# Up and gate products of three feed-forward layers by Strassen's scheme, their weight sums made by adding DMAs, in a one-core transformer kernel

## Chip, cores and metric

One core of a Trainium2 chip runs the whole kernel. The metric is the device time of one execution in microseconds (us); of several runs the median counts. PE is TensorE (matrix products), DVE VectorE, ACT ScalarE, POOL GpSimd, and SP SyncE, which issues the loads.

## What is computed

A two-layer diffusion trunk in float32 over 256 latent tokens (lat) and 256 context tokens (ctx), width D = 1024. Every layer is a half-step SwiGLU feed-forward (FFN), a token mixer, and a second FFN, each on normalised tokens with scale, shift and gate from a modulation vector:

```python
def swiglu(z, w13, w2):
    gate, up = jnp.split(z @ w13, 2, axis=-1)
    return (jax.nn.silu(gate) * up) @ w2
...
    for l in range(DEPTH):
        m_l = (s_lat @ mod_w[l] + mod_b[l]).reshape(b, N_MOD, 1, d)
        m_c = (s_ctx @ mod_w[l] + mod_b[l]).reshape(1, N_MOD, 1, d)
        h = h + 0.5 * m_l[:, 2] * swiglu(modulate(h, norm_g[l, 0], m_l[:, 0], m_l[:, 1]), ffn_w13[l, 0], ffn_w2[l, 0])
        hc = hc + 0.5 * m_c[:, 2] * swiglu(modulate(hc, norm_g[l, 0], m_c[:, 0], m_c[:, 1]), ffn_w13[l, 0], ffn_w2[l, 0])
```

The hidden width is 2816, which is 22 tiles of 128. The FFNs are named (layer, which): (0,0), (0,1) and (1,0) have all 512 tokens, (1,1) has the 256 latent ones. The mixer of layer 0 joins a spatial gate and grouped-query attention; that of layer 1 is a matrix LSTM. The modulation weights `mod_w` are 1024 x 9216 for each layer.

## The kernel before

Features lie on partitions, tokens on the free axis. Each float32 product is made of three matmuls of a faster type: every operand is split into a high and a low part, and `mm3` (lines 106 to 110) adds hi·hi, hi·lo and lo·hi. Weights come by loads that SP issues in program order into `raw` (pool `rawp`, four buffers of 1 MB). `wsplit` takes 128 x 1024 elements: ACT casts the high part (`whi`, line 102), DVE subtracts it to get the low part (`wlo`, line 103). The pool `whp` holds four such splits. A load waits until its buffer has been read, a cast until its `whi` buffer has been used by PE.

In `ffn` the work of an FFN with 512 tokens is:

- Column pairs: 11 values of `cc`, each with 256 columns of gate and 256 of up. A hidden tile of 128 columns takes 8 feature blocks x 3 matmuls of 128x512 for gate, and as many for up; so a column pair has 96 such matmuls. `hidden` (lines 518 to 521) makes silu(gate)·up and splits it into `hh` and `hl`.
- The first column pair of the FFNs (0,1) and (1,0) is done in two halves of 256 tokens, since the context half of `z` is ready later. Pieces of the norm before lie between its products (`poke`, `settle`).
- The second product, `w2`: four passes `dp` of 256 output columns over all 22 hidden tiles; the last pass in two token halves. `resid` (line 399) adds the result to `hT`.

DVE has a filler that lies between the other work: `mod_round_dve` makes 512 columns of the modulation (a round) out of two 1 MB loads by 16 DVE operations, then PE sums over the partitions (line 267). `fill` issues one eighth of a round, two operations; `tick` says how many eighths come per step, from `FILL`. `LEAD` lets the scheduler put the filler early.

The engines each run their queue in order; a scheduler sets the order ahead of time, from the order in which the code is written and from its priorities. The FFNs stand in this order:

```python
    filler.extend([(0, r) for r in range(4, 18)] + [(1, r) for r in range(18)])
    nxt = Next(0, 1)
    until[0] = (0, 17)
    ffn(0, 0, z, T, [(0, T)], nxt, fill13=FILL[0][0], fill2=FILL[0][1], first=first)
```

## Time and profile before

| what | value |
|---|---|
| time, median of 3 runs (lowest to highest) | 1754.0 us (1753.57 to 1755.47) |
| span of the profiled execution | 1753.2 us |
| PE busy | 1732.7 us, 99% |
| DVE busy | 1126.9 us, 64% |
| ACT busy | 635.0 us, 36% |
| POOL busy | 88.1 us, 5% |
| mean granted TensorE clock | 0.997 |
| moved by DMA | 256.90 MB, 147 GB/s |

The span runs from the first to the last instruction of the profiled execution. The lowest of the three times lies 0.4 us above it, the median 0.8 us. Matmuls are pipelined: in the rows each lasts longer than the distance to the next, and the distance is what a matmul costs in a row of them.

### The profile page before, as it was taken

To read this page: it belongs to the slowest core of one execution; us is meant where nothing else is said; L and a number is where in the kernel's file an instruction comes from. 1 tells how busy PE (TensorE), PEld (TensorE's weight loads), DVE (VectorE), ACT (ScalarE), POOL (GpSimd) and SP (SyncE) were. 2 spreads that over 40 slices of the span, in tenths; PEclk is the share of its full clock that TensorE was granted. 3 is DMA by queue.
4 is the path that set the end of the run, shared out by engine and by line. 5 is a ranking of instruction groups with operands and counts; after the bars stand their busy time and mean duration, and the time that the engine had idled before them with its cause. 6 is when DMAs were issued, how large, how long until landed. Compare 5 with 4: busy or idle time off the path is not lost.

```text
span 1753.2 us, 25482 instructions
## 1 busy us (share of the span) xinstructions
PE 1732.7 (99%) x10359; PEld 1470.2 (84%) x10359; DVE 1126.9 (64%) x1968; ACT 635.0 (36%) x1028; POOL 88.1 (5%) x109
## 2 busy tenths in 40 slices
PE   7999999999999999999999999999999999999998
PEld 5777777779988987777777987777889999899998
DVE  5677777767775676675676766663334965695554
ACT  4322222224665332222222432222223564364442
POOL 0000000001542000000000000000000001100000
PEclk9999999999999999999999999999999999999999
DMA  9655555555211234445454455443224432146552
GB/s 281 216 194 172 174 191 172 179 189 174 73 49 49 97 129 164 164 144 190 141 182 163 159 168 168 144 162 121 88 87 118 146 114 79 49 130 207 190 178 67
DMA packets 234937, 256.90 MB, mean 147 GB/s; under 512 B 9288, under 2 KB 201028, under 8 KB 234820
## 3 DMA queue, kind: packets, MB, share of 16 engines
q1 hardware_dynamic: 234788, 255.27, 45.0%
q8 instruction: 81, 1.33, 0.3%
q14 instruction: 36, 0.29, 0.1%
q10 hardware_dynamic: 32, 0.01, 0.0%
HBM read 254.21 MB, written 1.05 MB: 146 GB/s over the span
## 4 chain that ended last, share of the span: by engine, by line
PE 84%; issue 11%; DVE 2%; DMA 1%; ACT 1%; SPq 0%; POOL 0%; POOLq 0%; DVEq 0%; ACTq 0%
PE ps L108 23%; PE ps L110 23%; PE ps L109 23%; PE ps L659 2%; PE ps L660 2%; PE ps L661 2%; PE mod_ps L267 2%; DMA mod<-in_mod_w_dram 1%; PE nd_ps L1353 1%; PE pv_ps L995 1%; PE sc_ps L950 1%; PE nd_ps L1350 1%; PE prT_ps L113 1%; DVE wlo L103 1%; PE mod_ps L219 0%
## 5 line engine op out<-in xcount | busy, mean ns | idle before, releaser
L102 ACT CAST whi<-raw 128x1024 fp32r<-128x1024 f32 (+1 forms) x338 | 346.7, 1027 | 900.4 <-PE ps L109 792.8
L103 DVE TENSOR_TENSOR wlo<-raw,whi 128x1024 fp32r<-128x1024 f32 (+1 forms) x338 | 401.6, 1193 | 278.3 <-ACT whi L102 276.4
L108 PE MATMUL ps<-zhi,whi 128*128 128x512 f32 (+2 forms) x1616 | 575.3, 357 | 1.6 <-ACT zhi L366 1.6
L110 PE MATMUL ps<-zhi,wlo 128*128 128x512 f32 (+2 forms) x1616 | 574.2, 356 | 0.0
L109 PE MATMUL ps<-zlo,whi 128*128 128x512 f32 (+2 forms) x1616 | 573.4, 355 | 0.0
L108 PEld LDWEIGHTS ps<-zhi,whi 128*128 128x128 f32 x1616 | 304.6, 189 | 57.8 <-issue 10.6
L109 PEld LDWEIGHTS ps<-zlo,whi 128*128 128x128 f32 x1616 | 304.9, 189 | 46.2 <-issue 0.4
L110 PEld LDWEIGHTS ps<-zhi,wlo 128*128 128x128 f32 x1616 | 304.3, 189 | 44.6 <-issue 0.6
L258 DVE SCALAR_TENSOR_TENSOR mod_acc<-raw,s_st,mod_acc 128x512 f32<-128x512 f32 x448 | 305.7, 744 | 11.4 <-DMA raw<-in_mod_w_dram 11.3
L108 PE MATMUL ps<-hh,whi 128*128 128x256 f32 (+1 forms) x836 | 281.8, 337 | 0.0
L110 PE MATMUL ps<-hh,wlo 128*128 128x256 f32 (+1 forms) x836 | 281.7, 337 | 0.0
L109 PE MATMUL ps<-hl,whi 128*128 128x256 f32 (+1 forms) x836 | 280.8, 336 | 0.0
L110 PEld LDWEIGHTS ps<-hh,wlo 128*128 128x128 f32 x836 | 157.4, 188 | 21.9 <-issue 4.9
L108 PEld LDWEIGHTS ps<-hh,whi 128*128 128x128 f32 x836 | 157.5, 188 | 20.9 <-issue 4.1
L109 PEld LDWEIGHTS ps<-hl,whi 128*128 128x128 f32 x836 | 157.5, 188 | 19.6 <-issue 2.5
L519 DVE TENSOR_TENSOR sil<-sil,ps 128x512 f32<-128x512 f32 (+1 forms) x85 | 52.9, 623 | 139.9 <-PE ps L110 139.0
L659 PE MATMUL ps<-whi,zhi 128*128 128x256 f32 x288 | 82.4, 286 | 1.4 <-DVE cy L1056 1.4
L660 PE MATMUL ps<-wlo,zhi 128*128 128x256 f32 x288 | 80.8, 281 | 0.0
L661 PE MATMUL ps<-whi,zlo 128*128 128x256 f32 x288 | 80.8, 281 | 0.0
L119 POOL TENSOR_TENSOR rs<-rs,mhalf 128x2 f32<-128x2 f32 x12 | 8.5, 710 | 1069.0 <-DVE rs L118 1069.0
L659 PEld LDWEIGHTS ps<-whi,zhi 128*128 128x128 f32 x288 | 54.1, 188 | 2.6 <-ACT whi L102 1.8
L660 PEld LDWEIGHTS ps<-wlo,zhi 128*128 128x128 f32 x288 | 54.2, 188 | 0.4
(290 smaller groups left out, 1520.2 us busy)
## 6 DMA issues: line engine op xcount, KB each, us to landing
raw<-in_ffn_w_dram SPq DMA_DIRECT2D x103, 1024.0 KB, 5.3
raw<-in_mod_w_dram SPq DMA_DIRECT2D x64, 1024.0 KB, 7.4
raw<-in_ffn_w_dram SPq DMA_DIRECT2D x38, 896.0 KB, 5.0
raw<-in_ml_w_in_dram SPq DMA_DIRECT2D x12, 1024.0 KB, 5.7
mod<-in_mod_w_dram SPq DMA_DIRECT2D x16, 512.0 KB, 7.5
raw<-in_ab_w_in_dram SPq DMA_DIRECT2D x7, 1024.0 KB
raw<-in_ml_w_out_dram SPq DMA_DIRECT2D x4, 1024.0 KB, 5.5
raw<-in_ffn_w_dram SPq DMA_DIRECT2D x8, 256.0 KB, 3.0
```

Source lines behind the costliest of these rows:

```text
L102: act.copy(hi, view)
L103: dve.tensor_tensor(lo, view, hi.bitcast(F32), op=ALU.subtract)
L108: pe.matmul(ps, ah, bh, start=start, stop=False)
L109: pe.matmul(ps, ah, bl, start=False, stop=False)
L110: pe.matmul(ps, al, bh, start=False, stop=stop)
L113: pe.transpose(out_ps, in_sb, ident[:n, :n])
L258: dve.scalar_tensor_tensor(acc[:, v], raw[:, k], s1, acc[:, v], op0=ALU.mult, op1=ALU.add)
L267: pe.matmul(ps[32 * j : 32 * (j + 1), :256], onehot[:, MAXG - 1 - m : MAXG + 31 - m], acc[:, v, hf * 256 : (hf + 1) * 256], start=(m == 0) ...
L519: dve.tensor_tensor(sil[:, :N], sil[:, :N], pu[:, :N], op=ALU.mult)
L659: pe.matmul(o, zh, wh[:, k % 4], start=(k == 0), stop=False)
L660: pe.matmul(o, zh, wl[:, k % 4], start=False, stop=False)
L661: pe.matmul(o, zl, wh[:, k % 4], start=False, stop=(k == KD - 1))
```

## The change

For the three FFNs with 512 tokens `ffn512` takes the place of `ffn`. From the second column pair on (in (0,0) from the fourth), the 256 columns of gate and of up, the two halves of the features and the two halves of the tokens form a 2 x 2 block product. It is made of seven block products instead of eight (a form of Strassen's scheme): 28 column pairs in all. A block product is 24 matmuls of 128x256 (4 feature blocks x 3 parts x 2 column tiles). So a column pair has 168 matmuls of 128x256.

For that the weights need sums of blocks: a1, S3, S2 and S4 stand one after the other in the same half of the buffer `rsum`. Each is split, and then POOL issues a DMA that loads the next block from memory and adds it in place (two DMAs of 256 KB for a sum, six for a column pair). S1 is added on DVE, from the other half of `rsum` and from `rpl`, which holds the blocks a2 and g2 as they are. The tokens need sums too (`combos_lat`, `combos_ctx`, `combos_last`), made once for each FFN on DVE and ACT in two buffers of `rawp`, `zlat` and `zctx`.

The hidden tiles go in two chunks, 12 and 10: the column pairs of a chunk, then its part of `w2` in blocks of four hidden tiles (512 KB loads, 24 matmuls of 128x512). Before the first chunk's `w2` the next column pair has its buffers already (`rsum`, `rpl`, two splits). `hT` is added to twice.

Six modulation rounds of layer 0 are made on PE straight from the loaded weights (`mod_direct`): two after the first chunk's column pairs of (0,0), four after the second's. The filler keeps the other rounds; in layer 1 those from the tenth on are made for the latent tokens alone, by 8 operations instead of 16.

```diff
-FILL = ((4, 4), (3, 3.5), (3, 3.5))
-GROUPS = (((4, 6), (6, 10), (10, 18)), ((0, 4), (4, 6), (6, 18)))
+FILL = ((3, 2.5, 2), (3, 2.5, 2), (3, 2.5, 2))
+GROUPS = (((6, 10), (10, 12), (16, 18)), ((0, 4), (4, 6), (6, 10), (10, 18)))
+LATROUND = (1, 10)
+DIRECT = ((4, 5), (12, 13, 14, 15))
+SOFF = 6
+NWH = 4
+NSIL = 3
+CHUNKS = ((0, 12), (12, 22))
...
-                    s1 = s_st[:, 4 * kh + k, v : v + 1]
+                for v in range(nv):
+                    s1 = s_st[:, 4 * kh + k, SOFF + v : SOFF + v + 1]
                     if kh == 0 and k == 0:
                         dve.tensor_scalar(acc[:, v], raw[:, k], s1, None, op0=ALU.mult)
                     else:
                         dve.scalar_tensor_tensor(acc[:, v], raw[:, k], s1, acc[:, v], op0=ALU.mult, op1=ALU.add)
-                yield
+                    if nv == 2 and v == 1 or nv == 1 and k % 2 == 1:
+                        yield
...
+    def mod_direct(l, rounds):
+        n = len(rounds)
+        ps = abank("mdir_ps")
+        for m, r in enumerate(rounds):
+            raws = [wraw(mod_w[l], 4 * kh, 4, r * 512, 512) for kh in range(2)]
+            for i in range(2):
+                for j in range(4):
+                    k = 2 * j + i
+                    pe.matmul(
+                        ps[32 * j : 32 * (j + 1), :],
+                        s_st[:, k, SOFF - 2 * m : SOFF + 32 - 2 * m],
+                        raws[k // 4][:, k % 4],
+                        start=(m == 0 and i == 0),
+                        stop=(m == n - 1 and i == 1),
+                        tile_position=(0, 32 * j),
+                    )
+        sb = tmp.tile([P, T], F32, tag="sil", name="mdir_sb", bufs=NSIL)
+        act.copy(sb, ps)
...
+    def ffn512(l, i, z, nxt, rates, first=None, direct=None):
...
+            def combos_lat():
+                t = rawp.tile([P, 2, 4, HT], F32, tag="raw", name="zlat", bufs=4)
+                for n, ks in enumerate((lo4, hi4)):
+                    dve.tensor_tensor(t[:, n], z[0][:, ks, lat].bitcast(F32), z[1][:, ks, lat].bitcast(F32), op=ALU.add)
+                zf["lat"] = t
...
+            def combos_ctx():
+                t = rawp.tile([P, 2, 4, HT], F32, tag="raw", name="zctx", bufs=4)
+                for n, ks in enumerate((lo4, hi4)):
+                    dve.tensor_tensor(t[:, n], z[0][:, ks, ctx].bitcast(F32), z[1][:, ks, ctx].bitcast(F32), op=ALU.add)
+                b11, b21 = (zf["lat"][:, n] for n in range(2))
+                b12, b22 = (t[:, n] for n in range(2))
+                dve.tensor_tensor(b11, b11, b12, op=ALU.subtract)
+                dve.tensor_tensor(b12, b22, b12, op=ALU.subtract)
+                dve.tensor_tensor(b22, b22, b11, op=ALU.add)
+                act.mul(mov["T2"][0], b22, -1.0)
...
+                split_to(mov["T3"], b12)
+                dve.tensor_tensor(b21, b22, b21, op=ALU.subtract)
+                split_to(mov["T4"], b21)
+                zf["T1"] = b11
+            def combos_last():
+                split_to(mov["T1"], zf["T1"])
...
+            class Pair:
+                def __init__(self, cc):
+                    self.cc = cc
+                    self.w = {}
+                    r = rawp.tile([P, 2048], F32, tag="raw", name="rsum", bufs=4)
+                    self.x, self.y = (r[:, n * 1024 : (n + 1) * 1024].rearrange("p (k c) -> p k c", c=256) for n in range(2))
+                    nc.sync.dma_start(out=self.x, in_=src(cc, 0, 0))
+                    nc.sync.dma_start(out=self.y, in_=src(cc, 1, 0))
+                def plain(self):
+                    r = rawp.tile([P, 2048], F32, tag="raw", name="rpl", bufs=4)
+                    self.a2, self.g2 = (r[:, n * 1024 : (n + 1) * 1024].rearrange("p (k c) -> p k c", c=256) for n in range(2))
+                    nc.sync.dma_start(out=self.a2, in_=src(self.cc, 0, 1))
+                    nc.sync.dma_start(out=self.g2, in_=src(self.cc, 1, 1))
+                def add(self, t, u, kh):
+                    for ks in (slice(0, 2), slice(2, 4)):
+                        pool.dma_start(out=t[:, ks], in_=src(self.cc, u, kh)[:, ks], accum_op=ALU.add)
+                def split(self, n):
+                    view = {"a1": self.x, "S3": self.x, "S2": self.x, "S4": self.x, "S1": self.y}.get(n)
+                    if n == "S1":
+                        dve.tensor_tensor(self.y, self.y, self.g2, op=ALU.add)
+                    if view is None:
+                        view = self.a2 if n == "a2" else self.g2
+                    self.w[n] = wsplit(view, 4, 256, hp if n == "S3" else None)
+                    nxt_add = {"a1": (1, 0), "S3": (1, 1), "S2": (0, 1)}.get(n)
+                    if nxt_add:
+                        self.add(self.x, *nxt_add)
...
+            def product(ps, w, m, fresh):
+                wh, wl = w
+                mh, ml = mov[m]
+                for j in range(2):
...
+                    for k in range(4):
+                        for n, (a, b) in enumerate(((wh, mh), (wh, ml), (wl, mh))):
+                            pe.matmul(
+                                o,
+                                a[:, k, cs],
+                                b[:, k],
+                                start=fresh and j == 0 and k == 0 and n == 0,
+                                stop=j == 1 and k == 3 and n == 2,
+                                skip_group_check=True,
+                            )
...
+            def pair_products(pr, nx, f):
+                a, b, c = bank("pa"), bank("pb"), abank("pc")
+                w = pr.w
+                pr.split("S1")
+                product(a, w["a1"], "B11", True)
+                s1 = sil_tile("s1")
+                act.copy(s1, a)
+                pr.split("a2")
+                product(b, w["S2"], "T2", True)
+                dve.tensor_tensor(s1, s1, b, op=ALU.add)
+                if nx:
+                    nx.split("a1")
+                product(c, w["S1"], "T1", True)
+                pr.split("g2")
+                product(b, w["S3"], "T3", True)
...
+                dve.tensor_tensor(s7, s1, b, op=ALU.add)
+                dve.tensor_tensor(s7, s7, c, op=ALU.add)
+                if nx:
+                    nx.split("S3")
...
+                product(a, w["a2"], "B21", False)
+                act.activation(s7, s7, AF.Silu, scale=-1.0)
+                pr.split("S4")
+                product(b, w["g2"], "T4", False)
+                s4 = sil_tile("s4")
+                dve.tensor_tensor(s4, s1, b, op=ALU.add)
+                act.activation(s4, s4, AF.Silu, scale=-1.0)
+                if nx:
+                    nx.split("S2")
+                product(c, w["S4"], "B22", False)
+                dve.tensor_tensor(s4, s4, a, op=ALU.mult)
+                store(f, 2, s4, lat)
+                dve.tensor_tensor(s1, s1, c, op=ALU.add)
+                dve.tensor_tensor(s7, s7, s1, op=ALU.mult)
+                store(f, 2, s7, ctx)
+            def begin(pr):
+                pr.split("a1")
+                pr.split("S3")
+                pr.plain()
+                pr.split("S2")
...
+            else:
+                rg, ru = load_cc(0)
+                ws = [wsplit(r[:, :, j * P : (j + 1) * P], KD, P) for j in range(2) for r in (rg, ru)]
...
+                for n, ts in enumerate((lat, ctx)):
+                    ko = KD if n == 0 else KD // 2
...
+                    if n == 0:
+                        combos_lat()
+                    else:
+                        settle()
+                        combos_ctx()
+                        pr = Pair(cc)
+                    for a, k in order:
+                        if a == 0 and k in POKES:
+                            poke()
...
+                combos_last()
+                begin(pr)
+                for j in range(2):
+                    hidden(j, pss[2 * j], pss[2 * j + 1])
...
+            for ch, (f0, f1) in enumerate(CHUNKS):
+                while cc * 2 < f1:
+                    more = (cc + 1) * 2 < KF
+                    nx = Pair(cc + 1) if more else None
+                    pair_products(pr, nx, cc * 2 - f0)
+                    if more:
+                        nx.plain()
+                    pr = nx
+                    cc += 1
+                    tick(rates[1])
+                if direct is not None:
+                    mod_direct(l, direct[ch])
+                if ch == 0:
+                    dve.tensor_scalar(gate, mvec(l, 2 + 6 * i), 0.5, None, op0=ALU.mult)
+                nk = f1 - f0
+                blocks = [(k, min(4, nk - k)) for k in range(0, nk, 4)]
+                for dp in range(KD // 2):
...
+                        v = r.rearrange("p (k c) -> p k c", c=256)
+                        nc.sync.dma_start(
+                            out=v,
+                            in_=w2[l, i][(f0 + k0) * P : (f0 + k0 + n) * P, dp * 256 : (dp + 1) * 256].rearrange(
+                                "(k p) c -> p k c", p=P
+                            ),
+                        )
+                        return wsplit(v, n, 256)
...
+                    kept = {}
+                    for half, ts in enumerate((lat, ctx) if last else (slice(0, T),)):
+                        for k0, n in blocks:
+                            if k0 not in kept:
+                                kept[k0] = load_block(k0, n)
+                            wh, wl = kept[k0]
...
+                            if not last:
+                                tick(rates[2] * n / 4)
...
+                        for j in range(2):
+                            resid(acc if ch else None, dp * 2 + j, pss[j][:, ts], ts.start, ts.stop - ts.start, gate)
+                        if last:
+                            nxt.half(acc, half)
...
     HALVES = [(0, HT), (HT, T)]
-    filler.extend([(0, r) for r in range(4, 18)] + [(1, r) for r in range(18)])
+    filler.extend([(0, r) for r in range(6, 18) if r not in DIRECT[1]] + [(1, r) for r in range(18)])
     nxt = Next(0, 1)
     until[0] = (0, 17)
-    ffn(0, 0, z, T, [(0, T)], nxt, fill13=FILL[0][0], fill2=FILL[0][1], first=first)
+    ffn512(0, 0, z, nxt, FILL[0], first=first, direct=DIRECT)
     z = nxt.z
     nxt = Next(0, 2)
     with tc.tile_pool(name="em", bufs=1) as em:
@@ -1494,11 +1837,11 @@
     z = nxt.z
     nxt = Next(1, 0)
     until[0] = (1, 17)
-    ffn(0, 1, z, T, HALVES, nxt, fill13=FILL[1][0], fill2=FILL[1][1])
+    ffn512(0, 1, z, nxt, FILL[1])
     z = nxt.z
     nxt = Next(1, 1)
     until[0] = (1, 17)
-    ffn(1, 0, z, T, HALVES, nxt, fill13=FILL[2][0], fill2=FILL[2][1])
+    ffn512(1, 0, z, nxt, FILL[2])
```

Three places in the queues follow. Names with numbers are tiles; a row's `xN` means N alike in a row.

DVE's queue before, from the last context operations of the norm ahead of FFN (0,1) (`zlo`) to the first low parts of its second column pair (`wlo`):

```order
L367 SCALAR_TENSOR_TENSOR zlo_5422<-nt_5697,modT0_123,zhi_5421 128x256
L258 SCALAR_TENSOR_TENSOR mod_acc_5934<-raw_5935,s_st_119,mod_acc_5934 128x512
L256 TENSOR_SCALAR mod_acc_5934<-raw_5935,s_st_119 128x512
L258 SCALAR_TENSOR_TENSOR mod_acc_5934<-raw_5935,s_st_119,mod_acc_5934 128x512 x4
...
L258 SCALAR_TENSOR_TENSOR mod_acc_5934<-raw_6008,s_st_119,mod_acc_5934 128x512 x3
L103 TENSOR_TENSOR wlo_5872<-raw_5867,whi_5871 128x1024
```

The same place of DVE's queue now. `zlat`, `zctx`, T2l, T3l and T4l are the token sums; wlo_6589 is a1, xlo_6595 is S3, wlo_6604 is S2, wlo_6628 is S1:

```order
L413 SCALAR_TENSOR_TENSOR zlo_6126<-nt_6410,modT0_123,zhi_6125 128x256
L723 TENSOR_TENSOR zlat_6328<-zlat_6328,zctx_6474 128x1024
...
L727 SCALAR_TENSOR_TENSOR T2l_6299<-zctx_6474,T2h_6298 128x1024
L110 TENSOR_TENSOR wlo_6589<-rsum_6487,whi_6588 128x1024
...
L110 TENSOR_TENSOR xlo_6595<-rsum_6487,xhi_6594 128x1024
L772 TENSOR_TENSOR rsum_6620<-rsum_6620,rpl_6846 128x1024
L110 TENSOR_TENSOR wlo_6604<-rsum_6487,whi_6603 128x1024
L110 TENSOR_TENSOR wlo_6628<-rsum_6487,whi_6627 128x1024
```

Where filler and one low part stood, eight operations on token sums stand ahead of a1's low part, and the low parts of S3 and S2 each read `rsum` after another adding DMA.

SP's queue now, at the end of the first chunk's column pairs of FFN (0,0): the next pair's buffers (`rsum_1475`, `rpl_1701`), then the loads of a filler round and of the two rounds on PE (`raw`, lines 96), then those of `w2` (`raw2`):

```order
L756 DMA rsum_1475<-in_ffn_w13_dram 128x4x256
L757 DMA rsum_1475<-in_ffn_w13_dram 128x4x256
L762 DMA rpl_1701<-in_ffn_w13_dram 128x4x256
L763 DMA rpl_1701<-in_ffn_w13_dram 128x4x256
L96 DMA raw_1710<-in_mod_w_dram 128x4x512
L96 DMA raw_1717<-in_mod_w_dram 128x4x512
L96 DMA raw_1719<-in_mod_w_dram 128x4x512
L96 DMA raw_1729<-in_mod_w_dram 128x4x512
L96 DMA raw_1731<-in_mod_w_dram 128x4x512
L934 DMA raw2_1754<-in_ffn_w2_dram 128x4x256
```

PE's queue now at the same place: the last matmul of the last column pair (line 788), the two rounds (line 311), their transposes (line 120), and the first product of `w2` (line 115):

```order
L788 MATMUL pc_1480<-zhi_127,wlo_1634 128x256
L311 MATMUL mdir_ps_1716<-raw_1717,s_st_119 32x512 x2
L311 MATMUL mdir_ps_1716<-raw_1719,s_st_119 32x512 x2
...
L311 MATMUL mdir_ps_1716<-raw_1729,s_st_119 32x512 x2
L311 MATMUL mdir_ps_1716<-raw_1731,s_st_119 32x512 x2
...
L120 MATMUL mdirT_ps_1743<-ident_76,mdir_sb_1741 128x128 x4
L115 MATMUL ps_1752<-hh_737,whi_1756 128x512
```

Between the last column pair and `w2` PE now reads four 1 MB loads directly; with `rsum_1475` and `rpl_1701` held, two of the four `rawp` buffers are left for them and for `raw2`.

## Rows read from the trace of the kernel before

**Rows 1.** The page: span, engines, DMA.

```profile
span 1753.2 us, 25482 instructions
...
PE 1732.7 (99%) x10359; PEld 1470.2 (84%) x10359; DVE 1126.9 (64%) x1968; ACT 635.0 (36%) x1028; POOL 88.1 (5%) x109
...
DMA packets 234937, 256.90 MB, mean 147 GB/s; under 512 B 9288, under 2 KB 201028, under 8 KB 234820
```

**Rows 2.** Chain that ended last: shares of the span by engine.

```profile
PE 84%; issue 11%; DVE 2%; DMA 1%; ACT 1%; SPq 0%; POOL 0%; POOLq 0%; DVEq 0%; ACTq 0%
```

**Rows 3.** Groups by shape, PE: count, busy us, mean ns, idle before.

```profile
L108 PE MATMUL ps<-zhi,whi 128*128 128x512 f32 x1040 | 412.0, 397 | 1.6 <-ACT zhi L366 1.6
```

**Rows 4.** Timeline of PE, from 300 us: start, duration; first and last of 53.

```profile
299.79 0.39 PE L110 MATMUL ps<-hh,wlo 128*128 128x512 f32 x1
...
311.87 0.40 PE L108 MATMUL ps<-hh,whi 128*128 128x512 f32 x1
```

**Rows 5.** Timeline of PE, 1700 to 1705 us: first and last of 44.

```profile
1699.81 0.28 PE L108 MATMUL ps<-hh,whi 128*128 128x256 f32 x1
...
1704.92 0.28 PE L109 MATMUL ps<-hl,whi 128*128 128x256 f32 x1
```

**Rows 6.** Timeline of PE, 645.5 to 649.9 us, around a round's sum.

```profile
648.07 0.39 PE L110 MATMUL ps<-zhi,wlo 128*128 128x512 f32 x1
648.38 0.64 PE L267 MATMUL mod_ps<-mod_acc,onehot 128*32 128x256 f32 x8
...
649.29 0.39 PE L109 MATMUL ps<-zlo,whi 128*128 128x512 f32 x1
```

**Rows 7.** Timeline of DVE, 598 to 640 us: start, duration, idle before.

```profile
602.92 3.48 DVE L103 TENSOR_TENSOR wlo<-raw,whi 128x1024 fp32r<-128x1024 f32 x3
...
614.90 0.88 DVE L367 SCALAR_TENSOR_TENSOR zlo<-nt,modT,zhi 128x256 fp32r<-128x256 f32 x2
...
616.75 6.04 DVE L258 SCALAR_TENSOR_TENSOR mod_acc<-raw,s_st,mod_acc 128x512 f32<-128x512 f32 x9
```

**Rows 8.** Timeline of DVE, 280 to 360 us.

```profile
288.05 0.69 DVE L519 TENSOR_TENSOR sil<-sil,ps 128x512 f32<-128x512 f32 x1
288.64 1.09 DVE L103 TENSOR_TENSOR wlo<-raw,whi 128x896 fp32r<-128x896 f32 x1
```

**Rows 9.** Groups by shape, ACT.

```profile
L102 ACT CAST whi<-raw 128x1024 fp32r<-128x1024 f32 x262 | 274.9, 1051 | 672.4 <-PE ps L109 583.8 <-issue 63.1 <-DMA raw<-in_ffn_w_dram 11.0
```

**Rows 10.** DMA issues: count, KB each, median us to landing.

```profile
raw<-in_ffn_w_dram SPq DMA_DIRECT2D x103, 1024.0 KB, 5.3
raw<-in_mod_w_dram SPq DMA_DIRECT2D x64, 1024.0 KB, 7.4
...
mod<-in_mod_w_dram SPq DMA_DIRECT2D x16, 512.0 KB, 7.5
...
raw<-in_ffn_w_dram SPq DMA_DIRECT2D x8, 256.0 KB, 3.0
raw<-in_ab_w_out_dram SPq DMA_DIRECT2D x4, 512.0 KB, 3.7
raw<-in_ab_w_out_dram SPq DMA_DIRECT2D x8, 256.0 KB, 4.9
```

**Rows 11.** DMA, 280 to 360 us in 40 slices.

```profile
GB/s 0 231 293 0 265 348 355 348 187 12 0 0 78 377 74 209 367 386 336 143 0 8 0 9 246 269 22 310 355 366 367 88 0 0 44 360 120 15 287 369
```

**Rows 12.** Timeline of PE, 622 to 628 us, in FFN (0,1).

```profile
625.87 0.29 PE L110 MATMUL ps<-zhi,wlo 128*128 128x256 f32 x1
626.00 0.40 PE L108 MATMUL ps<-zhi,whi 128*128 128x512 f32 x1
```

**Rows 13.** Timeline of PE, 20 to 31 us.

```profile
25.52 0.63 PE L109 MATMUL ps<-zlo,whi 128*128 128x512 f32 x1
25.95 0.63 PE L110 MATMUL ps<-zhi,wlo 128*128 128x512 f32 x1
```

**Rows 14.** Sums of waits: us in total, times, longest us.

```profile
ACT whi L102 <- PE ps L109: 792.8, 247, 7.6
```

175 lines of the change are left out of this document (148 added, 27 removed).

## The prediction

> **What bounds the kernel now.** The page comes first: the span is 1753.2 us, PE is busy for 1732.7 of it and DVE for 1126.9 [rows 1], and the chain that ended last lies on PE for 84% and on its issue for 11% [rows 2]. So time is won only where PE does less, and it is lost wherever PE is made to wait, since hardly any slack is left in its queue. The groups show where PE's time is: the hi·hi part of the products with `z` alone has 1040 matmuls of 128x512, 412.0 us as the rows count them [rows 3]. Their length there (0.40 us) is no price, because they overlap. The price is the distance between starts: from 299.79 to 311.87 lie 52 distances, 0.2323 us each [rows 4]; for 128x256, from 1699.81 to 1704.92, 43 distances of 0.1188 us [rows 5], a little over half. The waits show who follows whom: ACT's casts wait 792.8 us in all for PE to free a split [rows 14]. So weights are ready early everywhere; this lead is what the change spends.
>
> **What PE saves.** A column pair has 96 x 0.2323 = 22.30 us now and 168 x 0.1188 = 19.96 us then: 2.34 us less, in 28 pairs 65.6 us. In `w2` the last pass of a 512-token FFN is 264 matmuls of 256 columns; then 120 of them and 72 of 512 columns: 144 x 0.1188 - 72 x 0.2323 = 0.38 us less, in three FFNs 1.1 us. A round's sum on PE takes the stretch from 648.07 to 649.29, where one matmul would take 0.23 and there are two: about 0.76 us more [rows 6]; six rounds less are 4.6 us. Together **71.3 us** less work on PE.
>
> **A pair in the middle of a chunk.** Prices on DVE, by distances again: a low part of 128x1024 1.13 us (3.48 for three, with their overlap), two filler operations 1.35 us (6.04 for nine, 0.67 each) [rows 7], an operation on 128x512 0.6 us (288.05 to 288.64) [rows 8]. A pair has seven low parts and the S1 sum (9.0 us), nine operations of 128x512 (5.4 us), and 2.5 filler steps (3.4 us): 17.8 us in 19.96. DVE fits, but with little to spare. The chain through POOL is what can be late: a1's low part, an add, the split of S3 (cast 1.05 us [rows 9], low part 1.13 us), an add, the split of S2. From DVE's order a1's low part ends some 5.6 us into the pair before, and S2 is wanted 2.85 us (24 matmuls) into its own, at 22.8 us. So 5.6 + 2 L + 2 x 2.2 must stay under 22.8: an add may take **L = 6.4 us**. Each microsecond beyond costs 2 us a pair, 56 in all. No row shows a DMA issued by POOL or one that adds. The nearest are loads by SP: 256 KB in 3.0 or 4.9 us, 512 KB (an add's two halves) in 3.7 or, behind others, 7.5 us [rows 10]. I take 5 us, between the two for 256 KB and room for issuing two; bounds 3.0 and 7.5. At 5 the chain leaves 2.8 us, and for queueing behind the filler I count 4 us in all 28 pairs (0 to 14).
>
> The Trainium skill bears on this in two places. "DMA: Bandwidth & Descriptors", section "Anatomy of one DMA", gives about 2.0 us plus bytes over 436 GB/s for a DMA from GpSimd: an estimate of 2.6 us for 256 KB, and nothing for the adding; by it the chain has still more room and the 4 us would be 0. "SBUF — State Buffer", in its box on DVE blocking DMA, says that such a DMA's descriptors are starved while DVE runs an operation that takes both port pairs, and cites 620 ns grown to 3100 ns; no row here can show it. What late adds do is the second rival below.
>
> **The start of (0,1) and (1,0).** Now PE goes from the halves to full width without a gap (625.87, 626.00) [rows 12], since only one low part stands in DVE's way. Then eight token sums stand between the last `zlo` (at 615.8 [rows 7]) and a1's low part: with one more ahead, ten operations of 1.13 us, so it is ready at 627.1; PE had its last work until 626.0. The first product runs to 630.0. The second needs S2: 627.1 + 2 (5 + 2.2) = 641.5. PE waits 1.1 and 11.5 us, **13 us at each start, 26 us in all**. With L at 3.0 it is 9 each, at 7.5 18 each. In (0,0) the sums lie beside three plain hidden tiles (3 x 48 x 0.2323 = 33 us of PE), so nothing is lost there.
>
> **The rounds on PE in (0,0).** Two `rawp` buffers are held by the next pair. The round's second load (raw_1719) needs a buffer that DVE's filler still reads: two adds and five filler operations behind the last product, 1.2 + 3.4 = 4.6 us; it lands 5.3 us later [rows 10], at 9.9. Only after that round's matmuls come the next two loads, 5.3 us and 2.9 us for the second megabyte (at 360 GB/s, the upper level in [rows 11]): 18.1. Then the first load of `w2`, 3.7 us, and its cast, 1.05: PE goes on at 22.9 us. In the second chunk no pair is ahead, but eight megabytes go through four buffers; the last four are issued about when the last product ends and land at 5.3 + 3 x 2.9 = 14.0, then 512 KB of `w2` and a cast: 16.5 us. Sum **39 us**. Bounds: at 2.9 us for each megabyte throughout, 16 + 14 = 30; with the 7.4 us of the modulation's loads [rows 10], 30 + 22 = 52.
>
> **`w2` of the first chunk.** A block of four tiles is 24 x 0.2323 = 5.57 us on PE. With one buffer left for `raw2`, when a filler load has the other, a block needs 3.7 + 1.05 + 1.13 = 5.9 us. That is 0.3 us in each of 36 blocks, 11 us; in (1,0) a filler load comes for almost every block (half the operations, the same bytes), so I take **15 us**, 0 if two buffers are always there, 45 with loads of 4.9 us.
>
> **The rest.** After a long wait PE may run slower for a while: at the start of the trace, 512 columns are 0.43 us apart (25.52, 25.95) [rows 13] against 0.23. Four long waits, each followed by some 5 us of matmuls at that distance, would cost up to 9 us; I take 4. The second addition to `hT` (16 operations for each FFN, about 0.44 us each as `zlo` [rows 7]) and the extra 42 MB lie beside PE: 297 MB at 147 GB/s now, against peaks of 386 [rows 1, 11]. If DVE's room in the pairs is gone, the additions would cost their 21 us.
>
> **Sum.** -71.3 + 4 + 26 + 39 + 15 + 4 = +16.7 us on the span of 1753.2: 1769.9, and 0.8 us from the span to the median gives **1771 us**. In words: what PE saves in 28 pairs is given back at eight places where a pipeline that used to be full has to be filled again.
>
> **Rivals.** (a) *The waits around the rounds on PE are hidden* (faster). The place is PE's queue between the last pair and `w2`; the price is 39 us. If the loads come under the pair's own products, because the filler's buffer comes free before the last product ends, only the two loads beyond the buffers remain, some 5 us: 1771 - 34 = 1737 us. It turns at 22 us for both together (39 less the 17 of the sum). For it speaks that the loads leave long stretches free (11 of 40 slices are under 13 GB/s [rows 11]); against it, that the buffers, not the loads, set the time. With the lower bounds elsewhere too (starts 18, `w2` 0, pairs and clock 0) it would be 1706. (b) *Adds are late.* At L = 7.5 us the pairs lose 2 x 1.1 x 28 = 62 us and the starts 10 more: 1771 + 72 - 4 = 1839. It decides nothing of the sign, only the size; for it speaks that the row with traffic around it has 7.5 us, against it that the loads with a free queue have 3.0. (c) *The products of 256 columns don't keep their distance* with three accumulators in turn: at 0.1327 us a column pair is as long as before, and the 65.6 us are gone: 1837. Against it speak [rows 5]: 43 distances with a new weight at every matmul.
>
> **Chances.** The sum as worked out, 1757 to 1795: 0.42. (a) with lower bounds, 1700 to 1750: 0.36. (b) 1795 to 1850: 0.16. (c) 0.02. About no change: 0.04. A measurement of this kernel can tell 0.2%, 3.5 us, from nothing. So faster 0.36, same 0.04, slower 0.60. The range is 1712 to 1836, for both signs hold much of the chance; the likeliest case alone has 1757 to 1795.
>
> **What would show it.** In the changed kernel's profile: PE's busy time below 1680 us with its share well under 99%; 128x256 of the block products 0.119 us apart; an idle PE of 10 us or more ahead of the first S2 product of (0,1) and (1,0); 23 and 17 us between the last block product and the first `w2` matmul in (0,0), part of them the rounds; waits of PE for DVE's low parts of S2 in the pairs close to zero; adds landing in about 5 us. The prediction is wrong if the adds take over 6.4 us, if the loads for the rounds on PE land under the products, or if DVE falls behind in the pairs.

## The result, and the profile after

The changed kernel takes 2279.1 us (median of 4 runs, 2277.26 to 2281.63) against 1753.9 us: 1.2985 times as long, with a 95% interval of 1.2967 to 1.3003. The forecast was 1771 us; it had the direction, and missed 508 of the 525 us.

The page of the changed kernel, as [rows 1], with the granted clock in tenths for 40 slices and the queue of POOL's DMAs (packets, MB, share of the span of 16 DMA engines):

```profile
span 2275.5 us, 30038 instructions
PE 1799.0 (79%) x12185; PEld 1597.0 (70%) x12185; DVE 1286.5 (57%) x2131; ACT 726.5 (32%) x1137; POOL 295.0 (13%) x277
...
PEclk9977798879999967879978987877987799999999
...
q1 hardware_dynamic: 227668, 246.63, 33.4%
q0 software_dynamic: 45696, 44.05, 14.0%
```

PE is idle for 476.5 us instead of 20.5, and yet busy for longer than before, although its queue holds less work. (Without the adds the same matmuls are busy for 1722.3 us; the kernel is in the next section.) The granted clock shows why: wherever the block products stand, it is at 0.6 to 0.8.

The sums of PE's waits (total us, times, longest) name the place:

```profile
PE pb L788 <- ACT whi L109: 320.0, 25, 23.4
PE ps L115 <- ACT whi L109: 46.2, 10, 19.2
PE mdir_ps L311 <- DMA raw<-in_mod_w_dram: 32.5, 6, 22.8
```

`pb` is the bank of the product that needs S2, the second of a pair; in 25 of 28 pairs PE waits for its split, 12.8 us on average. What the split waits for is seen in POOL's queue, at the start of FFN (0,1) (start, length, and in brackets the idle time before it):

```profile
793.04 1.29 POOL L767 DMA_DIRECT2D rsum<-in_ffn_w_dram  x1 [20.20 <-DVE wlo L110]
800.64 1.22 POOL L767 DMA_DIRECT2D rsum<-in_ffn_w_dram  x1 [6.31 <-DMA rsum<-in_ffn_w_dram]
808.00 1.22 POOL L767 DMA_DIRECT2D rsum<-in_ffn_w_dram  x1 [6.14 <-DVE xlo L110]
812.92 1.20 POOL L767 DMA_DIRECT2D rsum<-in_ffn_w_dram  x1 [3.71 <-DMA rsum<-in_ffn_w_dram]
820.34 1.21 POOL L767 DMA_DIRECT2D rsum<-in_ffn_w_dram  x1 [6.22 <-DVE wlo L110]
825.38 1.20 POOL L767 DMA_DIRECT2D rsum<-in_ffn_w_dram  x1 [3.82 <-issue]
830.35 1.22 POOL L767 DMA_DIRECT2D rsum<-in_ffn_w_dram  x1 [3.77 <-issue]
835.81 1.21 POOL L767 DMA_DIRECT2D rsum<-in_ffn_w_dram  x1 [4.25 <-DMA rsum<-in_ffn_w_dram]
```

ACT's casts of the finished sums S3 and S2, from its timeline:

```profile
805.28 1.04 ACT L109 CAST xhi<-rsum 128x1024 fp32r<-128x1024 f32 x1 [9.33 <-DMA rsum<-in_ffn_w_dram]
...
817.63 1.99 ACT L109 CAST whi<-rsum 128x1024 fp32r<-128x1024 f32 x2 [11.30 <-DMA rsum<-in_ffn_w_dram]
```

The two halves of an add are never under way together. The second starts about 4.9 us after the first, even where nothing but "issue" holds it (825.38 behind 820.34), and none of the 168 halves starts before the one ahead of it has landed. So these two adds take 12.2 us (793.04 to 805.28) and 9.6 us (808.00 to 817.63), not 5; over all 84 the median from the first issue to the second landing is 9.5 us. A half lands 4.6 us after its issue, by the median of the DMA issues:

```profile
rsum<-in_ffn_w_dram POOLq DMA_DIRECT2D x168, 256.0 KB, 4.6
```

Six halves are 6 x 4.9 = 29.4 us; two waits of POOL for the splits of S3 and S2, 2.9 us each, make 35.2. Two first products of neighbouring pairs, by ACT's copies of their result, lie 36.3 us apart instead of 20 (33 to 41 inside a chunk, 50 to 64 behind the first pair of three chunks):

```profile
859.47 0.58 ACT L813 COPY s<-pa 128x512 f32<-128x512 f32 x1
...
895.74 0.57 ACT L813 COPY s<-pa 128x512 f32<-128x512 f32 x1
```

What PE does meanwhile, first in its timeline, then in stretches of 2 us (length, PE busy, granted clock, DMA share, GB/s):

```profile
795.05 0.28 PE L788 MATMUL pa<-zhi,wlo 128*128 128x256 f32 x1
818.73 0.58 PE L788 MATMUL pb<-T2h,whi 128*128 128x256 f32 x1 [23.40 <-ACT whi L109]
```

```profile
794.00:796.00 2.00, 1.33 (x12) 1.00 1.09 342
...
798.00:800.00 2.00, 0.00 (x0) 0.50 1.13 292
...
820.00:822.00 2.00, 2.00 (x11) 0.50 0.05 12
...
828.00:830.00 2.00, 2.00 (x19) 1.00 0.83 142
```

While PE idles, the clock is granted at half (1.2 of 2.4 GHz), and the first products after the wait run at that level: 11 matmuls in 2 us instead of 19 in the rows' count. This answers to [rows 13].

Where the time went, by stages (from the first matmul of a stage to the first of the next, in PE's timelines; the last columns are two kernels of the next section, the one without adds and the one with chunks of 10 and 12 tiles):

| stage, us | before | after | without adds | best version |
|---|---|---|---|---|
| FFN (0,0) | 402.1 | 560.1 | 433.7 | 412.5 |
| FFN (0,1) | 388.9 | 550.3 | 381.0 | 370.9 |
| FFN (1,0) | 377.5 | 570.8 | 394.9 | 371.0 |
| the rest | 584.7 | 594.3 | 594.4 | 590.3 |
| span | 1753.2 | 2275.5 | 1804.0 | 1744.7 |

### The profile page after: what moved, and what is told of

It reads as the page before. It is cut to its first block, busy times and chain, and to the rows that moved or that the text cites. A ratio compares the mean times of both kernels' runs of the same rounds, so it can differ in the third digit from the quotient of the medians.

```text
span 2275.5 us, 30038 instructions
## 1 busy us (share of the span) xinstructions
PE 1799.0 (79%) x12185; PEld 1597.0 (70%) x12185; DVE 1286.5 (57%) x2131; ACT 726.5 (32%) x1137; POOL 295.0 (13%) x277
## 3 DMA queue, kind: packets, MB, share of 16 engines
q1 hardware_dynamic: 227668, 246.63, 33.4%
q0 software_dynamic: 45696, 44.05, 14.0%
## 5 line engine op out<-in xcount | busy, mean ns | idle before, releaser
L767 POOL DMA_DIRECT2D rsum<-in_ffn_w_dram x168 | 204.8, 1219 | 1219.1 <-DVE wlo L110 566.9
L109 ACT CAST whi<-raw 128x1024 fp32r<-128x1024 f32 (+2 forms) x208 | 210.8, 1016 | 404.9 <-DMA raw<-in_ffn_w_dram 187.5
L110 DVE TENSOR_TENSOR wlo<-raw,whi 128x1024 fp32r<-128x1024 f32 (+2 forms) x208 | 244.4, 1182 | 148.4 <-ACT whi L109 147.2
L115 PE MATMUL ps<-hh,whi 128*128 128x512 f32 (+1 forms) x764 | 274.8, 360 | 45.3 <-ACT whi L109 45.2
L116 PE MATMUL ps<-hl,whi 128*128 128x512 f32 (+1 forms) x764 | 272.1, 356 | 0.0
L117 PE MATMUL ps<-hh,wlo 128*128 128x512 f32 (+1 forms) x764 | 268.5, 357 | 3.0 <-DVE wlo L110 2.8
L115 PE MATMUL ps<-zhi,whi 128*128 128x256 f32 (+2 forms) x720 | 220.4, 309 | 2.8 <-ACT zhi L412 1.7
L117 PE MATMUL ps<-zhi,wlo 128*128 128x256 f32 (+2 forms) x720 | 219.7, 308 | 1.7 <-DVE wlo L110 1.7
L116 PE MATMUL ps<-zlo,whi 128*128 128x256 f32 (+2 forms) x720 | 219.9, 307 | 0.0
L116 PEld LDWEIGHTS ps<-zlo,whi 128*128 128x128 f32 x720 | 136.4, 190 | 6.6 <-issue 0.4
```

The source lines that it names most:

```text
L109: act.copy(hi, view)
L110: dve.tensor_tensor(lo, view, hi.bitcast(F32), op=ALU.subtract)
L115: pe.matmul(ps, ah, bh, start=start, stop=False)
L116: pe.matmul(ps, ah, bl, start=False, stop=False)
L117: pe.matmul(ps, al, bh, start=False, stop=stop)
L767: pool.dma_start(out=t[:, ks], in_=src(self.cc, u, kh)[:, ks], accum_op=ALU.add)
```

## Experiments

**More memory for descriptors.** The kernel reserves 1024 bytes a partition for the descriptors of POOL's DMAs. Twice as much:

```diff
-            t = tmp.tile([P, HT], F32, tag="nt", name="nt", bufs=3)
+            t = tmp.tile([P, HT], F32, tag="nt", name="nt", bufs=2)
...
-    nc = _bacc.Bacc("TRN2", target_bir_lowering=False, num_devices=1, dynamic_dma_scratch_size=1024)
+    nc = _bacc.Bacc("TRN2", target_bir_lowering=False, num_devices=1, dynamic_dma_scratch_size=2048)
```

> One number is changed: the memory for the descriptors of POOL's DMAs, 2048 bytes for each partition instead of 1024 (and the buffer ring of the norm's small tiles is two deep instead of three, to make room). Theory A: in the changed kernel the two halves of an add run one after the other (starts about 4.9 us apart, an add of 9.6 to 12 us), because the descriptors of one half fill more than half of the memory, so the second half waits until the first has landed; six of them and two splits of 2.9 us make the 35 us of a pair. With twice the memory both halves are under way at once: an add of about 6 us, a pair of about 23 us, 1880 to 1950 us in all. Theory B: an adding DMA is slow in itself, or POOL writes descriptors slowly, whatever the memory: the halves stay 4.9 us apart, and the time stays within 2240 to 2290.

Measured: 2044.9 us, ratio 1.1651 (1.1617 to 1.1685). The halves now start 0.7 us apart, so both are under way at once; POOL's timeline merges them to "x2":

```profile
731.46 2.52 POOL L767 DMA_DIRECT2D rsum<-in_ffn_w_dram  x2 [15.89 <-DVE wlo L110]
741.07 2.45 POOL L767 DMA_DIRECT2D rsum<-in_ffn_w_dram  x2 [7.08 <-DVE xlo L110]
751.64 2.42 POOL L767 DMA_DIRECT2D rsum<-in_ffn_w_dram  x2 [8.12 <-DVE wlo L110]
```

From one add to the next, with the split between, it is 9.6 and 10.6 us, where it was 15.0 and 12.3 (793.04, 808.00, 820.34). So theory A holds for the serial halves, and 234 us go with them; theory B is out. But the time is 95 us above the expected range, and inside a chunk the pairs are mostly 25 to 32 us apart, not 23, so that is not all.

**One DMA for an add.** 4096 bytes (with the shorter ring `nt`, and the ring `sil` made one shorter too for room), and 512 KB at once:

```diff
-                    for ks in (slice(0, 2), slice(2, 4)):
+                    for ks in (slice(0, 4),):
```

> 4096 bytes for descriptors, and each add is one DMA of 512 KB instead of two of 256 KB. Theory A: one fixed latency for each add and a transfer twice as long, about 6.5 us, 1880 to 1950 us in all, close to the kernel with 2048 bytes. Theory B: the work for each byte sets the time, an add stays near 9 us and the kernel above 2150.

Measured: 1997.2 us, ratio 1.138 (1.134 to 1.1419). The DMA issues, and POOL's timeline over the adds for S3, S2, S4 and the next pair's S3:

```profile
rsum<-in_ffn_w_dram POOLq DMA_DIRECT2D x84, 512.0 KB, 6.2
```

```profile
719.74 1.38 POOL L767 DMA_DIRECT2D rsum<-in_ffn_w_dram  x1 [16.06 <-DVE wlo L110]
728.60 1.29 POOL L767 DMA_DIRECT2D rsum<-in_ffn_w_dram  x1 [7.49 <-DVE xlo L110]
737.84 1.28 POOL L767 DMA_DIRECT2D rsum<-in_ffn_w_dram  x1 [7.95 <-DVE wlo L110]
741.24 1.29 POOL L767 DMA_DIRECT2D rsum<-in_ffn_w_dram  x1 [2.13 <-DVE wlo L110]
```

A DMA of 512 KB lands in 6.2 us, as theory A said, but the time is 47 us above its range. Add and split take 9 us, and the next pair's first add comes 3.4 us (later 6.6 us: 759.28, 765.92) behind this pair's add for S4. From one S3 add to the next that is 9 + 9 + 3.4 to 6.6 = 21.5 to 24.7 us for the first two, and 26 to 28 for the next three; by ACT's copies the pairs inside a chunk are 24 to 31 us apart, 36 to 43 behind the first pair of three chunks. The 6.6 us come from DVE's queue, where the next pair's a1 (764.06) stands behind S2's low part (757.65), the low parts of S1 and a2, and five operations on products and hidden tiles, without a pause between them:

```profile
757.65 1.23 DVE L110 TENSOR_TENSOR wlo<-rsum,whi 128x1024 fp32r<-128x1024 f32 x1 [1.57 <-ACT whi L109]
...
764.06 1.22 DVE L110 TENSOR_TENSOR wlo<-rsum,whi 128x1024 fp32r<-128x1024 f32 x1
```

**No adds.** The adding DMAs are left out, and with them the sums S3, S2 and S4 (`for ks in ():`).

> The adding DMAs are left out, so S3, S2 and S4 are split from the block that is there already; the kernel doesn't compute the weight sums. Everything else is as in the changed kernel. Theory A (the adds are the cause of nearly all of the loss): pairs of 20 to 21 us, starts of (0,1) and (1,0) with 5 us idle instead of 13, so 1740 to 1790 us. Theory C (buffers, DVE or the rounds on PE lose a good part of it as well): above 1850.

Measured: 1804.2 us, ratio 1.028 (1.025 to 1.031), between the ranges of the two theories. So the adds cost 475 us, and 50 us of the loss are something else. Inside a chunk the pairs are 20 to 23 us apart (one 33). The engines' line of the page, and the rounds on PE of the first chunk in PE's timeline:

```profile
PE 1722.3 (95%) x12185; PEld 1534.8 (85%) x12185; DVE 1286.8 (71%) x2131; ACT 735.5 (41%) x1137; POOL 88.9 (5%) x109
```


```profile
166.44 1.05 PE L311 MATMUL mdir_ps<-raw,s_st 128*32 128x512 f32 x4
174.86 3.63 PE L311 MATMUL mdir_ps<-raw,s_st 128*32 128x512 f32 x12 [7.37 <-DMA raw<-in_mod_w_dram]
181.98 1.92 PE L311 MATMUL mdir_ps<-raw,s_st 128*32 128x512 f32 x4 [3.50 <-DMA raw<-in_mod_w_dram]
185.66 3.63 PE L311 MATMUL mdir_ps<-raw,s_st 128*32 128x512 f32 x12 [1.76 <-DMA raw<-in_mod_w_dram]
...
192.25 0.79 PE L115 MATMUL ps<-hh,whi 128*128 128x512 f32 x1 [1.16 <-ACT whi L109]
```

From 166.44 to 192.25 are 25.8 us (forecast 22.9); in the second chunk, from 373.85 to 392.34, 18.5 us (16.5). `w2` of the first chunks takes 78, 82 and 93 us, where its matmuls are 67.

**The sums by POOL's instructions.** All four blocks are in `rsum` and `rpl`, so nothing need be loaded again:

```diff
-                    for ks in (slice(0, 2), slice(2, 4)):
-                        pool.dma_start(out=t[:, ks], in_=src(self.cc, u, kh)[:, ks], accum_op=ALU.add)
+                    block = {(1, 0): "y", (1, 1): "g2", (0, 1): "a2"}[u, kh]
+                    pool.tensor_tensor(t, t, getattr(self, block), op=ALU.add)
...
                 pr.split("g2")
+                if nx:
+                    nx.plain()
```

> All four blocks of a pair are in rsum and rpl anyway; so POOL adds them with its own instructions on 128x1024 (about 2.5 us, from 1.29 us for 128x512 on POOL in the mixer) instead of loading them again; rpl is loaded a little earlier, behind the split of g2. Theory A: the chain of a pair is 5.6 + 2 x 2.5 + 2 x 2.2 = 15 us of 22.8, so no wait: 1745 to 1795 us, within 20 us of the kernel without adds. Theory D (POOL's additions and DVE's operations get in each other's way): pairs above 23 us and more than 1850 us.

Measured: 1918.0 us, ratio 1.0929 (1.0897 to 1.096): theory D. Inside a chunk the pairs are 23 to 27 us apart, and DVE's timeline shows why, beside POOL's:

```profile
698.23 3.43 DVE L801 TENSOR_TENSOR hl<-sil,hh 128x512 fp32r<-128x512 f32 x2
...
705.05 3.41 DVE L110 TENSOR_TENSOR wlo<-rpl,whi 128x1024 fp32r<-128x1024 f32 x1
708.38 1.21 DVE L110 TENSOR_TENSOR wlo<-rsum,whi 128x1024 fp32r<-128x1024 f32 x1
```

```profile
698.39 2.72 POOL L767 TENSOR_TENSOR rsum<-rsum,rpl 128x1024 f32<-128x1024 f32 x1 [2.42 <-DVE xlo L110]
704.01 3.36 POOL L767 TENSOR_TENSOR rsum<-rsum,rpl 128x1024 f32<-128x1024 f32 x1 [2.90 <-DVE wlo L110]
```

The low part that starts under POOL's second addition takes 3.41 us instead of 1.2 and ends 1.1 us behind it; the next one is normal. (The two operations of DVE's first line take 3.43 us beside POOL's first addition; in the changed kernel such two take 1.28.) The Trainium skill's page "SBUF — State Buffer" says in its section on two sides that GpSimd and a DVE operation with two SBUF inputs shut each other out while GpSimd reads; the rows agree. In all DVE was busy 104 us longer than without adds (1390.5 against 1286.8), 1.24 us for each of 84 sums: what a sum would cost on DVE itself.

**The sums on DVE.** The same with `dve.tensor_tensor`.

> As the kernel whose sums POOL adds by instructions, but on DVE: three operations of 1.13 us more for each pair. Theory E: POOL's and DVE's additions hinder each other (DVE was busy 104 us longer in that kernel, 1.24 us for each of the 84 sums, as much as a sum costs on DVE), so DVE alone does no worse: DVE has 21.2 us of work in a pair, pairs of 21.5 to 23 us, 1820 to 1870 us. Rival: what made those pairs 25 us is DVE's fill alone, then 1900 to 1950 us.

Measured: 1821.2 us, ratio 1.0376 (1.0346 to 1.0407), theory E, at the lower end of its range. DVE is busy 1373.3 us (1390.5 in the kernel with POOL's instructions), and inside a chunk the pairs are mostly 19 to 24 us apart. The sums and their order are those of the changed kernel, only `rpl` is loaded a little earlier; made on DVE they cost 17 us above the kernel without sums, not 475.

**Less fill in the pairs**, more in `w2`: `FILL = ((3, 1, 2.8), (3, 1, 2.8), (3, 1, 2))`.

> As the kernel with sums on DVE, with one filler step for each pair instead of 2.5, and 2.8 instead of 2 for each block of the second product in (0,0) and (0,1). Theory: DVE bounds the pairs; 2 us less there: 30 to 50 us less than the kernel before it, unless the blocks of the second product, now at 4.9 of 5.57 us of DVE, lose it again. Rival: DVE's waits, not its work, bound the pairs, and the time stays within 10 us.

Measured: 1837.2 us, 16 us slower than the kernel before it. Both expectations miss: the pairs gain little, and `w2` loses more (from the first matmul of `w2` to the next pair's, or to the end of the FFN, 78 us become 93 and 63 become 73 in (0,0)), which points to `w2` as the tight place.

**The next pair later.** Its buffers and splits are taken in the last of the first chunk's four passes of `w2`:

```diff
-                    nx = Pair(cc + 1) if more else None
+                    nx = Pair(cc + 1) if more and (cc + 1) * 2 < f1 else None
...
+                    ahead = ch == 0 and dp == KD // 2 - 1
+                    if ahead:
+                        pr = Pair(cc)
+                        pr.plain()
...
+                            if ahead:
+                                pr.split(("a1", "S3", "S2")[k0 // 4])
```

> As the kernel with less fill, but the pair after the first chunk's second product takes its buffers and splits only in the last of the four passes, not ahead of the first. Theory: the second product of the first chunks loses 11 to 26 us in each FFN, 53 in all in the kernel without adds, because that pair holds two of four load buffers and two of four splits; 25 to 45 us of it come back. Rival: the stalls there come from the filler's loads and sums; then less than 10 us.

Measured: 1773.0 us, ratio 1.0101 (1.0061 to 1.0142): 64 us less, more than expected. PE's timeline at the first chunk's rounds:

```profile
162.79 3.64 PE L311 MATMUL mdir_ps<-raw,s_st 128*32 128x512 f32 x32
...
169.70 0.50 PE L115 MATMUL ps<-hh,whi 128*128 128x512 f32 x1
```

The lump of 25.8 us (25.7 in the kernel before it) has shrunk to 6.9: all loads of the two rounds were there, and no buffer was held. `w2` of the first chunks, until the next pair's products, goes from 93, 97 and 93 us to 80, 74 and 74. The buffers and splits held by the next pair were the cause in both places.

**The rounds spread between the products**, half a round at a time, with the next load issued behind each half, and no fill in the pairs of (0,0):

```diff
+                next(dgen, None)
                 product(c, w["S1"], "T1", True)
...
                 product(a, w["a2"], "B21", False)
+                next(dgen, None)
```

> As the kernel with the late prefetch, but the six rounds on PE are done half a round at a time between the products of the pairs, each load issued one step ahead, and no filler in the pairs of (0,0). Theory: the two lumps cost 44 us in the kernel without adds, of which 18 are PE's own work; 20 to 30 us come back, and with all four changes the kernel lands between 1725 and 1775 us. Rival: the loads stand in the way of the pairs' own in the four buffers, and less than 10 us come back.

Measured: 1771.9 us, ratio 1.0095 (1.0066 to 1.0125). It lands in the expected range, but only 1 us came back and not 20 to 30: the rival's result. FFN (0,0) gains 2 us, some 6 in the second chunk with its `w2`, less some 4 in the first, whose `w2` has more fill now. One reason, which is not the rival's, is in PE's own rows. The matmuls of two rounds take 3.64 us in a lump (the 32 above): four of them, one for each of four strips of 32 output partitions, start within 0.03 us of each other, and the next four 0.43 us later. A half round has only two of the strips, so two start at a time, as far apart: its 8 take 1.84 us until the next product, and two rounds 7.4. A lump of 6.9 us could give nothing back by this. Then four rounds were spread and two kept in a lump, with the fill set for each chunk and two filler rounds moved to (0,1) (`until[0] = (0, 15)`):

> As the kernel with the late prefetch, but the four rounds of the second chunk of (0,0) are spread between its products (the two of the first chunk stay in one lump, which cost 7 us there), two layer-0 rounds of the filler move from (0,0) into (0,1), and the filler steps are set for each chunk (2 a pair, 2.3 to 2.6 a block; none in the pairs with spread rounds). Theory: the lump of the second chunk (18 us) and some 8 us of the second products of (0,0) come back: 1740 to 1760 us, about level with the kernel before. Rival: DVE is so full in pairs with two steps that they lose it, then 1765 to 1790 us.

Measured: 1778.0 us, ratio 1.0137 (1.012 to 1.0154), a miss: the moved rounds came due at the gate ahead of the first `w2` of (0,1), which took 86 us (74 in the kernel with the late prefetch).

**One more plain column pair** at the starts of (0,1) and (1,0), beside which the token sums lie:

```diff
+                whole_tile(2, rg, ru, 0)
+                combos_ctx()
+                pr = Pair(cc)
+                pr.plain()
+                combos_last()
+                pr.split("a1")
+                whole_tile(3, rg, ru, 1)
```

> As the kernel before it, with one more plain column pair at the start of (0,1) and of (1,0), so 26 pairs by seven products. Theory: the token sums then lie beside 22 us of plain products, and the 10 to 11 us that each start loses come back, less 2 x 2.3 us for the plain pairs: 12 to 17 us less than the kernel before it, so 1725 to 1745 us, below the kernel before the change. Rival: the start is bound by the buffers of the token sums, and at most 5 us come back.

Measured: 1767.2 us, ratio 1.0073 (1.0058 to 1.0088), 10.8 us less: short of the expected 12 to 17 and far above the expected time, since the kernel before it was slower than expected; the rival, at most 5, is out.

**Six rounds on PE**: `DIRECT = ((4, 5), (12, 13, 14, 15, 16, 17))`, three half rounds in a pair.

> As the kernel with one more plain pair, but the last two rounds of layer 0 are also made on PE, between the products of the second chunk of (0,0), instead of by DVE's filler in (0,1), where the gate waited for them ahead of the second product (that chunk's second product took 90 us instead of the 67 of its matmuls); the filler's steps are evened out (48 in (0,0), 56 in each of the others). Theory: 15 us come back in (0,1), 8 us of matmuls are added in (0,0): 1750 to 1762 us. Rival: the second products of the first chunks are slow for the buffers alone, and nothing comes back: 1765 to 1780 us.

Measured: 1757.2 us, ratio 1.0015 (1.0006 to 1.0025), as expected; `w2` of the first chunk of (0,1) is down from 90 to 72 us, which speaks for the gate's rounds as the cause (the fill was evened out as well).

**S4 by adding DMA** with S3 and S2 on DVE:

```diff
+                    if (u, kh) == (0, 1):
+                        for ks in (slice(0, 2), slice(2, 4)):
+                            pool.dma_start(out=t[:, ks], in_=src(self.cc, u, kh)[:, ks], accum_op=ALU.add)
+                        return
```

> As the kernel before it, but the sum S4 is made by the two adding DMAs of the changed kernel, with the same 1024 bytes for descriptors; S3 and S2 stay on DVE. Theory: an add of 10 to 12 us costs nothing where 14 us lie between S2's low part and the product that needs S4, and DVE has 1.1 us less in each pair: within 10 us of the kernel before it, to either side. Rival (the adding DMAs cost by their mere presence, by DVE or the loads that they slow down): 20 us or more slower.

Measured: 1765.6 us, ratio 1.0067 (1.0045 to 1.009), 8.4 us more: inside the theory's margin, but clear of noise. The serial halves are the same as in the changed kernel (4.8 us apart, by the median); without a chain behind them an add a pair costs 8 us in 26 pairs, where three in a chain cost 475 in 28.

**Chunks of 10 and 12 tiles**: `CHUNKS = ((0, 10), (10, 22))`, fill in (0,0) `(4, (2, 0), (2.4, 1.8))`.

> As the kernel with six rounds on PE, but the chunks are of 10 and 12 hidden tiles instead of 12 and 10 (and the filler's steps in (0,0) set to that). What is open: outside the three FFNs the changed kernel and all its variants take about 10 us more than the kernel before, in the mixers, whose code is the same. Theory: the last pass of w2, under which the next norm is prepared, has 10 hidden tiles instead of 22, 7 us for each token half instead of 16; with 12 tiles it has 8.6 us, so 1 to 2 us come back behind each of (0,0) and (1,0), 1751 to 1757 us. Rival: the mixers wait for something else (their weights, the modulation): no change there.

Measured: **1746.4 us, ratio 0.9953 (0.9939 to 0.9966)**, the best version: 0.5% below the kernel before, the whole interval below 1. Its page:

```profile
span 1744.7 us, 29416 instructions
PE 1709.5 (98%) x12091; PEld 1522.9 (87%) x12091; DVE 1334.5 (76%) x2157; ACT 729.0 (42%) x1128; POOL 87.3 (5%) x109
```

The two mixers with what follows them give back 1.4 and 2.7 us, about as the theory said; 6 us more come from (1,0), for which no run shows the reason, and 2 from (0,0), whose fill was changed too.

**All rounds spread**, the first two as well, with no fill in the pairs of (0,0) and 2.25 instead of 1.8 in its second `w2`:

> As the kernel before it, with the two rounds of the first chunk of (0,0) spread between its products as well. Theory: the lump costs 10 us, of which 4 are PE's own work; 4 to 6 us come back, 1746 to 1753 us, level with the kernel before the change or just below it. Rival: the spread rounds take a load buffer from the two pairs of that chunk, and nothing comes back.

Measured: 1751.5 us, ratio 0.9978 (0.9969 to 0.9986), not better than the lump. The rival's result came, but its reason is not shown. The lump, in the kernel before it and from the first of these rows to the second, was 6.8 us and not 10:

```profile
140.87 3.64 PE L311 MATMUL mdir_ps<-raw,s_st 128*32 128x512 f32 x32
...
147.66 0.50 PE L115 MATMUL ps<-hh,whi 128*128 128x512 f32 x1 [1.04 <-ACT whi L109]
```

The four half rounds that take its place cost 7.4 us of PE, by rows like the first of these two (until the second):

```profile
110.50 1.91 PE L347 MATMUL mdir_ps<-raw,s_st 128*32 128x512 f32 x8
112.34 0.38 PE L827 MATMUL pa<-zhi,whi 128*128 128x256 f32 x1
```

And the second `w2` of (0,0), with the fill that left the pairs, takes 78.2 us instead of 75.0. The profiled execution, the fastest of eleven, spans only 1 us more than that of the lump (1745.7 against 1744.7); where the others lose their time is not shown.

## Why the prediction was wrong

**The step that failed** first is the price of an add: "I take 5 us, between the two for 256 KB and room for issuing two; bounds 3.0 and 7.5". It took 9.5 us by the median, 9.6 and 12.2 us at the start of (0,1). The rows behind it were all loads issued by SP, and the two halves were taken to be under way together. They are not: they start 4.9 us apart. With twice the descriptor memory they start 0.7 us apart, so the memory is the cause. Rival (b), adds late, was therefore the right case, and the prediction had named adds above 6.4 us as a sign of being wrong; but its bound of 7.5 us was too low, and its price, 1839 us, by 440.

**The rule for what an add costs** failed as well. "Each microsecond beyond costs 2 us a pair" above 6.4 would give 2 x 3.2 x 28 = 179 us at 9.6; the adds cost 475. The chain was taken from one pair's a1 to its S2, while POOL's queue holds six serial DMAs a pair, S4's two among them: 35.2 us, near the 36.3 measured. And the 6.4 itself is too high: with one DMA that lands in 6.2 us the rule gives no loss, but that kernel takes 193 us more than the one without adds. There an add with its split takes 9 to 11 us and not 6.2 + 2.2, and the next a1's low part comes 6.4 us behind S2's (764.06, 757.65), where the prediction's 5.6 and 2.85 leave 2.75. With sums of 1.2 us on DVE the same order loses 17 us. How the 193 us divide between these two, and whether that kernel's shorter rings have a part in them, is not shown.

**The clock** was the third. While PE idles the granted clock falls to half, and the same matmuls were busy 77 us longer than without adds (1799.0 against 1722.3). The "4" for it was sized for four waits, not for one in nearly every pair. The rest of the difference of the two spans, 395 of 471.5 us, is idle time (476.5 against 81.7).

**What held, and what did not.** The distance of matmuls held: a block product's 24 keep 0.12 us, and inside a chunk the pairs of the kernel with the late prefetch are 20.1 us apart by the median, 0.1 above the 19.96. The sign named for the saving, PE busy below 1680 us, was not seen in any kernel: 1722.3 without adds, 1709.5 in the best version, which has 26 such pairs and two more rounds on PE. So the 71.3 us as a whole are not shown. Without adds the rounds on PE cost 44 us against the 39 forecast; in the first chunk the held buffers were the cause (6.9 us once they are free). The starts of (0,1) and (1,0) cost 26.1 and 26.8 us of waiting in the changed kernel (two waits each, the longer 23.4 and 21.1), twice the 13, by the long add. With the sums on DVE and the late prefetch the five pairs of those chunks still take 112.9 and 114.0 us, 13 and 14 above 5 x 19.96, though a sum is short there; so the starts lose by more than the add. Rival (a) did not come about, and (c) neither.

**What was missed beside it.** `w2` of the first chunks loses about 53 us without adds, where 15 were counted; holding two of four buffers and splits was the right cause, at a higher price (the late prefetch gives back 64 us, the lump's 19 among them). And the rest of the kernel takes 10 us longer, though its code is unchanged: the last pass of `w2` has 10 hidden tiles instead of 22, and the norm that is prepared under it has 7 us of cover for each half instead of 16. Chunks of 10 and 12 move it the expected way; that this explains all 10 us is argued, not shown.

## What to carry to other kernels

A DMA by another engine and of another kind has no price in the rows of plain loads: measure one by itself, and count how many can be under way at once, before a chain of three is built on it. Then follow the chain round, through every queue that it shares, until it meets its own start in the next pair. A pipeline that gives away its lead pays twice, in waiting and in the clock of what follows. Here 0.5% was won only after the sums had left the DMAs, the buffers held across a phase had been let go, and the starts and chunks had been set anew. Where two engines hinder each other on operands in SBUF, moving an operation to the idle one need not save anything: here the sums on POOL took 1918 us, on the busier DVE 1821.

## What the hardware showed that was not expected

Adding costs DMA time: in the changed kernel POOL's queue moved 44.05 MB in 14.0% of the span of 16 engines, 319 us, so 138 GB/s; the plain loads moved 246.63 MB in 33.4%, 760 us, 325 GB/s. The size of the packets is not the reason: in this trace one of 1024 bytes took 117 ns where it was added and 51 ns where it was not, on average. An adding DMA of 256 KB lands in 4.6 us alone; of two together both have landed 6.9 us after the first issue, and one of 512 KB lands in 6.2 us (all medians). From the Trainium skill's page "DMA: Bandwidth & Descriptors", section "Anatomy of one DMA", an estimate for 256 and 512 KB is 2.6 and 3.2 us; the measurement decides, and adding is not in that fit. Of the starving of POOL's descriptors by DVE, which the prediction cited from the Trainium skill's page "SBUF — State Buffer", the length of POOL's issues shows nothing: the 168 last 1.203 to 1.373 us. Their landings range from 4.3 to 10.5 us, and no run tells what held the long ones. A DVE operation on two SBUF operands of 1.2 us took 3.4 us when it began under a POOL operation that reads SBUF. And matmuls with 32 columns of weights for different strips of the output ran side by side: 32 in 3.64 us with four strips in turn, 8 in 1.84 us with two.
